# Taking 64 of 256 tokens out of the expert scans of a two-model kernel and gathering their expert rows by index

## The chip, the core and the metric

The kernel runs on one core of one Trainium2 chip. The metric is the time of one execution of the whole program in microseconds (us); the median of three runs is compared. The core has a matrix engine (PE, with its weight loads shown as PEld), three elementwise engines (DVE = VectorE, ACT = ScalarE, POOL = GpSimd), a queue for transfers (SP), and 16 DMA engines that all queues share.

## The reference, cut to what matters

Two transformer models run one after the other on 256 tokens of width 1024, two layers each. The change is in the last part of each layer of the first model, a layer of 16384 experts: every token picks 8 x 16 = 128 experts, takes the dot product of its normed input with each one's `down` row, and adds up their `up` rows, weighted.

```
def peer_ffn(x, w_query, sub_keys, down, up):
    ...
    idx = jnp.take_along_axis(cand_i, pos, axis=-1)     # per token 8 heads x 16 experts
    gate = jax.nn.softmax(top_s, axis=-1)

    def expert_block(args):
        xb, ib, gb = args
        a = jnp.einsum('thkd,td->thk', down[ib], xb).astype(jnp.float32)
        c = (gb * jax.nn.gelu(a)).astype(up.dtype)
        return jnp.einsum('thk,thkd->td', c, up[ib]).astype(x.dtype)
    ...
```

## The kernel before

Nothing is gathered before the change. The function `peer` computes the dot products of all 256 tokens with all 16384 `down` rows as a dense matrix product, multiplies them by a matrix of gates that is zero except where a token chose an expert, and multiplies the result with all `up` rows, again dense. All of this is in 32-bit floats split into two parts: a weight tile `wr` (128 x 1024, 512 KB) is fetched by SP, ACT rounds it to `wh` (line 255), DVE forms the rest `wl` (line 256), and `mm3` (lines 303 to 305) issues three matmuls for each 128 x 128 block. So one weight tile stands for 24 matmuls, with the 256 tokens as the moving columns. `wr`, `wh` and `wl` have four buffers each.

Four stages follow each other in each of the two layers, with 64 weight tiles each:

- **First down scan**, `dscan(0)`: the first 8192 `down` rows. Beside it DVE does the routing (the top-k, the indices `ij`, the gates `gt`).
- **Second down scan**, `dscan(1)`: the other 8192. Beside it `build(0)` makes the gates of the first half in 32 blocks of 8 tokens. A block is three fp16 operations on DVE (line 1314 twice, line 1329 once), 16 small fp16 matmuls of one-hot matrices (line 1338), and one multiply of `ga` on DVE (line 1320).
- **First up scan**, `uscan(0)`: `ga` of the first half times the `up` rows. Beside it `build(1)`. `coef` (lines 293 and 294) splits `ga` for two weight tiles at a time.
- **Second up scan**, `uscan(1)`: the rest of the `up` rows, with nothing beside it. `tail` then adds the sums `accs` to the residual.

What runs beside a scan is a generator. After each weight tile `wt` calls `tick`, which adds a rate to a credit and lets the generator issue work until the costs that it yields have used the credit up (`R1`, `R2`, `R3` = 1150, 1500, 1600 a tile; a block of `build` yields 600 + 900 + 600). Each engine works through its own queue in order, and an instruction that has to wait holds up everything behind it on that engine. POOL has no part in the work before the change.

Of the kernel before, what the change touches and what calls it, by code (L numbers as in the profile page):

```python
# [23 lines left out]
F32 = mybir.dt.float32  # L24
# [3 lines left out]
U32 = mybir.dt.uint32  # L28
AF = mybir.ActivationFunctionType
OP = mybir.AluOpType  # L30
# [90 lines left out]
def prep(inp):  # L121
# [11 lines left out]
    for l in range(DEPTH):  # L133
# [14 lines left out]
        a[f"sk{l}"] = bd  # L148
        a[f"down{l}"] = np.ascontiguousarray(
            i["peer_down"][l].reshape(128, 128, 8, 128).transpose(0, 3, 2, 1)).reshape(128, 128, 1024)  # L150
        a[f"up{l}"] = np.ascontiguousarray(i["peer_up"][l]).reshape(128, 128, 1024)

        w = i["w_in_2"][l]
# [44 lines left out]
class K:  # L198
    def __init__(self, ctx, tc, ap, ahead):
        self.tc, self.nc, self.ap, self.ctx = tc, tc.nc, ap, ctx  # L200
        nc = self.nc
        self.P = ctx.enter_context(tc.tile_pool(name="keep", bufs=1))
        self.W = ctx.enter_context(tc.tile_pool(name="wts", bufs=1))
        self.S = ctx.enter_context(tc.tile_pool(name="scr", bufs=1))
        self.ps = ctx.enter_context(tc.tile_pool(name="psum", bufs=1, space=PSUM))
        self.dr = ctx.enter_context(tc.tile_pool(name="dram", bufs=1, space=DRAM))
        self.x = self.P.tile([128, 8, T], F32, name="xres", bufs=1)
        self.nw = self.P.tile([128, 13, 8], F32, name="nw")
        self.eps = self.P.tile([128, 1], F32, name="eps")
# [20 lines left out]
        self.todo, self.sqs = [], []  # L230

    def cap(self, name, rows=128):
        o, w = _COFF[name]
# [31 lines left out]


    def tick(self):
        self.credit += self.rate
# [141 lines left out]
    def tail(self, accs, rows, wi, scale=None):  # L410

        self.pre(wi)
        if wi == N_FIN:
# [5 lines left out]
        def done(d):  # L419
            s = slice(2 * d, 2 * d + 2)  # L420
            xs = self.x[:, s]
            if scale is None:
# [11 lines left out]
        self.lastrows(accs, rows, done)  # L434
        if wi != N_FIN:
            self.todo = self.norm_steps()
            return
# [38 lines left out]
    def colpair(self, srcs, xh, xl):  # L476
# [636 lines left out]
WARM = 14  # L1113
R1, R2, R3 = 1150, 1500, 1600
H1 = H2 = 0


def peer(k, l, nxt):
# [4 lines left out]
    with k.tc.tile_pool(name=f"peer_{l}", bufs=1) as p:  # L1123
# [5 lines left out]
        ga1 = p.tile([128, HI * T], F32, name="ga1")  # L1129
        top = ExitStack()  # L1130
        q = top.enter_context(k.tc.tile_pool(name=f"first_{l}", bufs=1))
        ga = [q.tile([128, HI * T], F32, name="ga0"), ga1]

        rt, off = ga[1], [HI * T - 13000]

        def rtile(*shape):
            n = 1
# [1 line left out]
                n *= s  # L1139
            a = rt[:, off[0]:off[0] + n]  # L1140
            off[0] += n
            assert off[0] <= HI * T
# [12 lines left out]
        nc.sync.dma_start(sk, ap[f"sk{l}"])  # L1155
        k.cols(ap[f"w_q{l}"], 0, 8, xh, xl, lambda j, m, ps: V.tensor_mul(qT[:, j:j + m], ps, k.rsb))

        for h in range(0, 8, 2):
            for tt in range(2):
                ps = k.pst("mx", [128, 2, 256])  # L1160
                for j in range(2):
                    nc.tensor.matmul(ps[:, j], qT[:, h + j, tt * 128:(tt + 1) * 128], sk, start=True, stop=True)  # L1162
                c = h + tt
                t = k.S.tile([128, 2, T], F32, name="sq", bufs=2)[:, 0]
                V.scalar_tensor_tensor(t, k.x[:, c], k.nw[:, N_FFN + l, c:c + 1], k.rs, op0=OP.mult, op1=OP.mult)
                k.split(xh[:, c], xl[:, c], t)
                nc.scalar.copy(sc[:, tt, h:h + 2], ps)
        TB = 8
        room = k.P.tile([128, 4096], F16, name="xres", bufs=1)
        sizes = (TB * 128, TB * HI, 2 * TB * HI)  # L1170
# [5 lines left out]

        def dscan(half, dst):
            def ev(j, m, ps):
                nc.scalar.activation(dst[:, j * T:(j + m) * T], ps[:, :m].rearrange("p a t -> p (a t)"), AF.Gelu_apprx_tanh)  # L1179
            k.cols(down, half * HI, HI, xh, xl, ev)  # L1180


        sv = rtile(2, 8, 2, 16)
# [14 lines left out]
        def routing():  # L1198
# [79 lines left out]
            for src, kind in ((ij[0], 0), (ij[1], 1), (gt, 2)):  # L1278
# [8 lines left out]
                else:  # L1287
# [3 lines left out]
                    V.tensor_copy(g3[:, :, 0], gb)  # L1291
                    V.tensor_sub(g3[:, :, 1], gb, g3[:, :, 0])

        k.beside(routing(), R1, H1)
        dscan(0, ga[0])

        sets = [[room[:, starts[i]:starts[i + 1]] for i in range(3)],
                [k.S.tile([128, sizes[0]], F16, name="sq", bufs=2), room[:, starts[3] + sizes[0]:starts[3] + sizes[0] + sizes[1]],
# [1 line left out]
        pairs = io16.rearrange("p (a d) -> p a d", d=2)  # L1300

        def build(half, dst):
            d3 = dst.rearrange("p (i t) -> p i t", t=T)
            hs = slice(half * HI, (half + 1) * HI)

            def parts(b):
# [37 lines left out]
        dscan(1, ga[1])  # L1344
        k.drain()
        accs = k.rows_begin()
        ring = [k.S.tile([128, 8, T], F32R, name=n, bufs=1) for n in ("xh", "xl")]
        end = []

        def at(i):  # L1350
            return [t[:, i % 8] for t in ring] if i < 2 * HI - 2 else [t[:, i % 2] for t in end]

        def coef(i):
            r, o = i % 8, i % HI * T
            h, lo = [t[:, r:r + 2] for t in ring] if i < 2 * HI - 2 else end
            k.split(h.rearrange("p a t -> p (a t)"), lo.rearrange("p a t -> p (a t)"), ga[i // HI][:, o:o + 2 * T])

        def uscan(half):
            for i in range(half * HI, (half + 1) * HI, 2):
# [2 lines left out]
                if i % HI + 2 < HI:  # L1362
                    coef(i + 2)
                if i == 2 * HI - 2:
                    k.tail(accs, [k.wt(ap[f"up{l}"][e]) + tuple(at(e)) for e in (i, i + 1)], nxt, scale=1.0 / GS)
                else:
                    for e in (i, i + 1):
                        k.row(accs, *k.wt(ap[f"up{l}"][e]), *at(e), e == 0, False)

        k.beside(build(1, ga[1]), R3, H2)  # L1370
        uscan(0)
        k.drain()
        top.close()
# [391 lines left out]
```

## Time and profile before

| | us |
|---|---|
| runs (three) | 2913.3, 2915.08, 2918.97 |
| median | 2915.08 |
| the profiled execution | 2919.18 |
| its span, first to last instruction | 2917.1 |
| PE busy in the span | 2889.8 (99%) |
| DVE busy | 2077.0 (71%) |
| ACT busy | 1457.7 (50%) |
| POOL busy | 0.2 |

The four stages of the first layer lie at 243 to 1015 us, those of the second at about 1236 to 2013 us. Busy time of PE is the union of pipelined records, so a busy PE only says that it never ran dry; how fast it goes is read from the distance between the starts of two matmuls. The granted clock is 0.994 on average, and 1.00 (the level of 2.4 GHz) in the stages above.

### The profile page before, as it was taken

How to read it: one execution, taken by the hardware profiler on the slowest of the kernel's cores; microseconds unless marked ns; L12 is line 12 of the kernel's file. 1: busy time of each engine (PE TensorE's matmuls, PEld its weight loads, DVE VectorE, ACT ScalarE, POOL GpSimd, SP SyncE). 2: the span in 40 equal slices, each digit the busy share in tenths (PEclk: the TensorE clock that was granted, in tenths of full speed). 3: DMA queues.
4: the chain of work that ended last, by engine and by line, in shares of the span. 5: the costliest groups of instructions: out<-in, count | busy, mean ns of one | idle time of the engine just before them, and what ended most of it. 6: DMA issues, size and time to landing. Idle time of an engine off the chain costs nothing.

```text
span 2917.1 us, 59823 instructions
## 1 busy us (share of the span) xinstructions
PE 2889.8 (99%) x25130; PEld 2836.1 (97%) x25130; DVE 2077.0 (71%) x3484; ACT 1457.7 (50%) x1963; POOL 0.2 (0%) x4
## 2 busy tenths in 40 slices
PE   9999999999999999999999999999999999999998
PEld 8989999999999989999999999999999999999998
DVE  7769978769755586798786895556667656667655
ACT  7655553443444476545434434444546544546544
POOL 0000000000000000000000000000000000000000
PEclk9999999999999999999999999999999999999999
DMA  6655554554555555555545445555455555455553
GB/s 202 182 171 168 182 179 163 166 171 160 188 181 184 179 171 181 176 178 184 169 163 172 163 160 195 182 184 189 153 173 188 179 183 179 162 186 181 174 182 129
DMA packets 150493, 511.50 MB, mean 175 GB/s; under 512 B 17176, under 2 KB 26520, under 8 KB 149200
## 3 DMA queue, kind: packets, MB, share of 16 engines
q1 hardware_dynamic: 145904, 503.02, 53.2%
q10 hardware_dynamic: 4320, 4.67, 0.5%
q8 instruction: 196, 3.21, 0.5%
q14 instruction: 73, 0.60, 0.1%
HBM read 500.23 MB, written 7.39 MB: 174 GB/s over the span
## 4 chain that ended last, share of the span: by engine, by line
PE 95%; ACT 2%; DMA 1%; DVE 1%; issue 0%; SPq 0%; ACTq 0%; DVEq 0%
PE col L303 18%; PE col L305 18%; PE col L304 18%; PE acc L303 12%; PE acc L304 12%; PE acc L305 12%; PE mx L1338 2%; ACT wh L255 1%; PE mx L1162 1%; DMA wr<-in_w_hi 0%; PE acc L658 0%; PE acc L1402 0%; DVE wl L256 0%; PE mx L341 0%; DMA c_tri<-in_consts 0%
## 5 line engine op out<-in xcount | busy, mean ns | idle before, releaser
L255 ACT CAST wh<-wr 128x1024 fp32r<-128x1024 f32 (+1 forms) x922 | 960.3, 1044 | 1276.0 <-PE col L304 594.5
L256 DVE TENSOR_TENSOR wl<-wr,wh 128x1024 fp32r<-128x1024 f32 (+1 forms) x922 | 1120.4, 1217 | 608.1 <-ACT wh L255 605.4
L303 PE MATMUL col<-xh,wh 128*128 128x256 f32 x3856 | 1104.7, 286 | 2.3 <-ACT silg L1574 0.9
L305 PE MATMUL col<-xh,wl 128*128 128x256 f32 x3856 | 1096.1, 284 | 4.6 <-DVE wl L256 4.6
L304 PE MATMUL col<-xl,wh 128*128 128x256 f32 x3856 | 1094.7, 284 | 0.0
L305 PEld LDWEIGHTS col<-xh,wl 128*128 128x128 f32 x3856 | 741.7, 192 | 6.8 <-DVE wl L256 5.4
L303 PEld LDWEIGHTS col<-xh,wh 128*128 128x128 f32 x3856 | 742.0, 192 | 4.5 <-ACT silg L1574 1.7
L304 PEld LDWEIGHTS col<-xl,wh 128*128 128x128 f32 x3856 | 742.0, 192 | 0.1
L303 PE MATMUL acc<-xh,wh 128*128 128x256 f32 x2016 | 574.4, 285 | 2.1 <-ACT xh L293 2.1
L304 PE MATMUL acc<-xl,wh 128*128 128x256 f32 x2016 | 570.5, 283 | 0.0
L305 PE MATMUL acc<-xh,wl 128*128 128x256 f32 x2016 | 570.1, 283 | 0.0
L303 PEld LDWEIGHTS acc<-xh,wh 128*128 128x128 f32 x2016 | 386.4, 192 | 2.4 <-ACT xh L293 2.4
L304 PEld LDWEIGHTS acc<-xl,wh 128*128 128x128 f32 x2016 | 387.1, 192 | 0.0
L305 PEld LDWEIGHTS acc<-xh,wl 128*128 128x128 f32 x2016 | 386.9, 192 | 0.0
L1320 DVE TENSOR_TENSOR ga<-ga,mx 128x512 f32<-128x512 f32 x128 | 87.3, 685 | 41.5 <-PE mx L1338 39.5
L304 PE MATMUL acc<-fl,wh 128*128 128x256 f32 x352 | 98.1, 279 | 0.0
L305 PE MATMUL acc<-fh,wl 128*128 128x256 f32 x352 | 98.0, 279 | 0.0
L303 PE MATMUL acc<-fh,wh 128*128 128x256 f32 x352 | 97.7, 280 | 0.0
L294 DVE TENSOR_TENSOR xl<-ga,xh 128x512 fp32r<-128x512 f32 x126 | 85.7, 683 | 0.0
L293 ACT CAST xh<-ga 128x512 fp32r<-128x512 f32 x126 | 76.9, 615 | 0.0
L1179 ACT ACTIVATE ga<-col 128x512 f32<-128x512 f32 x128 | 75.7, 592 | 0.0
L303 PE MATMUL col<-wh,xh 128*128 128x512 f32 (+3 forms) x192 | 70.7, 372 | 3.4 <-ACT hg L1076 2.0
(466 smaller groups left out, 3420.0 us busy)
## 6 DMA issues: line engine op xcount, KB each, us to landing
wr<-in_down SPq DMA_DIRECT2D x256, 512.0 KB, 3.5
wr<-in_up SPq DMA_DIRECT2D x256, 512.0 KB, 3.9
wr<-in_w SPq DMA_DIRECT2D x132, 512.0 KB, 3.9
wr<-in_w_in SPq DMA_DIRECT2D x106, 512.0 KB, 4.0
wr<-in_xa_k SPq DMA_DIRECT2D x16, 512.0 KB, 4.0
wr<-in_xa_v SPq DMA_DIRECT2D x16, 512.0 KB, 4.3
wr<-in_w_out SPq DMA_DIRECT2D x16, 512.0 KB, 3.4
wr<-in_w_q SPq DMA_DIRECT2D x16, 512.0 KB, 3.5
```

The lines of the kernel that those rows point to most:

```text
L255: nc.scalar.copy(h[:, :w], r[:, :w])
L256: self.lows.append(nc.vector.tensor_sub(l[:, :w], r[:, :w], h[:, :w].bitcast(F32)).ins.name)
L293: self.nc.scalar.copy(h, src)
L294: self.nc.vector.tensor_sub(l, src, h.bitcast(F32))
L303: mm(ps, ah, bh, start=first, stop=False, skip_group_check=True)
L304: mm(ps, ah, bl, start=False, stop=False, skip_group_check=True)
L305: mm(ps, al, bh, start=False, stop=last, skip_group_check=True)
L1162: nc.tensor.matmul(ps[:, j], qT[:, h + j, tt * 128:(tt + 1) * 128], sk, start=True, stop=True)
L1179: nc.scalar.activation(dst[:, j * T:(j + m) * T], ps[:, :m].rearrange("p a t -> p (a t)"), AF.Gelu_apprx_tanh)
L1320: V.tensor_mul(dv, dv, ps.rearrange("p t i -> p i t"))
L1338: nc.tensor.matmul(ps[:, t], oj[:, t], gi[:, t, q], start=q == 0, stop=q == 1, skip_group_check=True)
```

## The change

Tokens 192 to 255 (`GN` = 64) leave the dense scans, which now have `TD` = 192 moving columns. For each of them the 128 chosen rows of `down` and of `up` are fetched by index. The 64 tokens x 128 experts are spread on 128 partitions, two partitions to a token, so there are `NG` = 64 gathers of 128 `down` rows (512 KB each) and 64 of `up` rows in each layer. A gather is an indirect DMA that POOL issues into one of four buffers `grow`. A `down` gather is reduced on DVE against the token's input `xg` (line 1367). Of each three `up` gathers two are scaled in place on ACT (line 1380) and added to `pacc` on POOL (line 1381), and one is scaled and added to `gacc` on DVE (line 1384). `gsel` then folds the two partitions of a token into `accs` with small matmuls (line 1449). A second generator, `other`, runs beside the first; its rate is `GR2` = 600 in the second down scan, `GR3` = 500 in the first up scan and `GR4` = 3000 in the second up scan, where a `down` row costs 1200, an `up` row for POOL 400 and one for DVE 1200. What is left is issued before the last sums.

```diff
     def tick(self):
+        if self.other is not None:
+            self.lent += self.orate
+            while self.other is not None and self.lent > 0:
+                c = next(self.other, None)
+                ...
+                    self.lent -= c
...
-                self.coltile(ps[:, j], h, l, xh, xl)
+                self.coltile(ps[:, j, :xh.shape[2]], h, l, xh, xl)
...
+GN = 64
+TD = T - GN
+RS = 128 // GN
+NG = 128 // RS
+NB = 4
+PSH = (2, 3)
+GR2, GR3, GR4 = 600, 500, 3000
...
-                k.split(xh[:, c], xl[:, c], t)
+                k.split(xh[:, c, :TD], xl[:, c, :TD], t[:, :TD])
+                nc.scalar.copy(t2[:, :128].rearrange("p (s t) -> p s t", s=RS), t[:, None, TD:].to_broadcast([128, RS, GN]))
+                nc.tensor.matmul(px[c // 4][:, c % 4 * 128:c % 4 * 128 + 128], t2[:, :128], k.ident, start=True, stop=True,
+                                 skip_group_check=True)
...
+        k.drain()
+
+        def gathered():
+            tabs = [ap[f"rows{l}"], ap[f"up{l}"].rearrange("a b c -> (a b) c")]
+            rows = []
+            def get(n):
+                if n < 2 * NG:
+                    r = p.tile([128, D], F32, name="grow", bufs=NB)
+                    nc.gpsimd.indirect_dma_start(out=r, out_offset=None, in_=tabs[n // NG],
+                                                 in_offset=bass.IndirectOffsetOnAxis(ap=gix[:, n % NG:n % NG + 1], axis=0))
+                    rows.append(r)
+            for n in range(NB - 1):
+                get(n)
+            for g in range(NG):
+                get(g + NB - 1)
+                r = rows.pop(0)
+                V.tensor_tensor_reduce(r, r, xg, 1.0, 0.0, OP.mult, OP.add, gav[:, g:g + 1])
+                ...
+                yield 1200
+            ...
+            for g in range(NG):
+                get(NG + g + NB - 1)
+                r = rows.pop(0)
+                c = gav[:, g:g + 1]
+                if PSH and g % PSH[1] < PSH[0]:
+                    nc.scalar.mul(r, r, c)
+                    nc.gpsimd.tensor_add(pacc, pacc, r)
+                    yield 400
+                else:
+                    V.scalar_tensor_tensor(gacc, r, c, gacc, op0=OP.mult, op1=OP.add)
+                    yield 1200
+        k.other, k.orate = gathered(), GR2
...
-            n = T // TB
+            n = TD // TB
...
+        def more(d):
+            if d == 0:
+                while k.other is not None:
+                    k.lent = 1e9
+                    k.tick()
+            gs = [gacc, pacc] if PSH else [gacc]
+            for j in range(2):
+                for i, g in enumerate(gs):
+                    nc.tensor.matmul(accs[d][:, j, TD:], g[:, (2 * d + j) * 128:(2 * d + j + 1) * 128], gsel, ...)
...
+            k.split(h[:, :, :TD], lo[:, :, :TD], ga[i // HI][:, o:o + 2 * TD].rearrange("p (a t) -> p a t", a=2))
...
         k.beside(build(1, ga[1]), R3, H2)
+        k.orate = GR3
         uscan(0)
...
+        k.orate = GR4
         uscan(1)
```

On ACT, where the second up scan of the first layer begins, before the change (`wr` to `wh` is a weight tile, `ga` to `xh` the rounding of coefficients for two tiles; numbers tell buffers apart):

```order
L293 CAST xh_7600<-ga0_2297 128x512
L255 CAST wh_10078<-wr_10076 128x1024
L255 CAST wh_10108<-wr_10106 128x1024
L293 CAST xh_7600<-ga0_2297 128x512
L255 CAST wh_10140<-wr_10138 128x1024
L293 CAST ch_10262<-ga1_2293 128x512
L255 CAST wh_10170<-wr_10168 128x1024
L293 CAST xh_7600<-ga1_2293 128x512
```

ACT alternates between weight tiles and coefficients, and goes on so to the end of the stage. On ACT a few tiles into the same stage after the change (`grow` is an `up` row for each partition, scaled in place by its weight `gav`):

```order
L257 CAST wh_10162<-wr_10160 128x1024
L257 CAST wh_10201<-wr_10199 128x1024
L303 CAST xh_7575<-ga1_2293 128x2x192
L1380 ACTIVATE grow_10172<-grow_10172,gav_2299 128x1024
L1380 ACTIVATE grow_10205<-grow_10205,gav_2299 128x1024
L1370 ACTIVATE gav_2299<-gav_2299 128x16
L257 CAST wh_10241<-wr_10239 128x1024
L1380 ACTIVATE grow_10247<-grow_10247,gav_2299 128x1024
L1380 ACTIVATE grow_10251<-grow_10251,gav_2299 128x1024
L257 CAST wh_10292<-wr_10290 128x1024
L303 CAST xh_7575<-ga1_2293 128x2x192
L1380 ACTIVATE grow_10258<-grow_10258,gav_2299 128x1024
```

The 43 scalings of the layer stand within 18 successive weight tiles, two or three ahead of each; behind them ACT's queue again has only weight tiles and coefficients.

On POOL, at the same place after the change (before it, POOL's queue held only its start-up):

```order
L1358 DMA grow_10169<-in_rows0,gix_2297 128x1024
L1358 DMA grow_10172<-in_up0,gix_2297 128x1024
L1358 DMA grow_10205<-in_up0,gix_2297 128x1024
L1381 ISA
L1381 TENSOR_TENSOR pacc_2296<-pacc_2296,grow_10172 128x1024
L1358 DMA grow_10208<-in_up0,gix_2297 128x1024
L1358 DMA grow_10247<-in_up0,gix_2297 128x1024
L1358 DMA grow_10251<-in_up0,gix_2297 128x1024
L1381 TENSOR_TENSOR pacc_2296<-pacc_2296,grow_10205 128x1024
L1358 DMA grow_10255<-in_up0,gix_2297 128x1024
L1358 DMA grow_10258<-in_up0,gix_2297 128x1024
L1381 TENSOR_TENSOR pacc_2296<-pacc_2296,grow_10247 128x1024
```

Gathers of `up` rows and the adds of earlier ones now share this queue, one behind the other: three gathers to two adds.

## Rows read from the trace of the kernel before

**Rows 1.** The page: busy time by engine, and the chain that ended last.

```profile
PE 2889.8 (99%) x25130; PEld 2836.1 (97%) x25130; DVE 2077.0 (71%) x3484; ACT 1457.7 (50%) x1963; POOL 0.2 (0%) x4
PE 95%; ACT 2%; DMA 1%; DVE 1%; issue 0%; SPq 0%; ACTq 0%; DVEq 0%
```

**Rows 2.** Stages of layer one: length, PE, PEld, DVE, ACT, POOL, clock, DMA share, GB/s.

```profile
246.00:430.00 184.00, 184.00 (x1548) 183.96 (x1547) 158.72 (x471) 93.27 (x104) 0.00 (x0) 1.00 0.57 184
430.00:626.00 196.00, 196.00 (x2006) 194.67 (x2005) 143.87 (x189) 80.19 (x94) 0.00 (x0) 1.00 0.52 167
626.00:815.00 189.00, 187.93 (x1920) 186.56 (x1917) 156.09 (x214) 80.28 (x95) 0.00 (x0) 1.00 0.53 171
830.00:1010.00 180.00, 180.00 (x1503) 180.00 (x1502) 94.21 (x92) 79.11 (x90) 0.00 (x0) 1.00 0.58 184
```

**Rows 3.** PE timeline (start, us): 256-column matmuls around four of one column.

```profile
208.73 0.28 PE L305 MATMUL col<-xh,wl 128*128 128x256 f32 x1
208.85 0.50 PE L341 MATMUL mx<-ones,sq 128*128 128x1 f32 x4
209.21 0.36 PE L303 MATMUL col<-xh,wh 128*128 128x256 f32 x1
209.41 0.28 PE L304 MATMUL col<-xl,wh 128*128 128x256 f32 x1
209.53 0.28 PE L305 MATMUL col<-xh,wl 128*128 128x256 f32 x1
```

**Rows 4.** Timeline of PEld, the weight loads of the same place.

```profile
208.74 0.53 PEld L341 LDWEIGHTS mx<-ones,sq 128*128 128x128 f32 x4
209.19 0.19 PEld L303 LDWEIGHTS col<-xh,wh 128*128 128x128 f32 x1
209.30 0.19 PEld L304 LDWEIGHTS col<-xl,wh 128*128 128x128 f32 x1
```

**Rows 5.** Timeline of PE: matmuls with 512 moving columns.

```profile
25.07 0.40 PE L303 MATMUL col<-wh,xh 128*128 128x512 f32 x1
25.77 0.40 PE L303 MATMUL col<-wh,xh 128*128 128x512 f32 x1
```

**Rows 6.** Timeline of PE: the 16 records of one block of gates.

```profile
429.18 0.64 PE L1338 MATMUL mx<-xres 128*128 128x64 f16 x16
429.66 0.36 PE L303 MATMUL col<-xh,wh 128*128 128x256 f32 x1
```

**Rows 7.** Timeline of DVE in the first up scan.

```profile
635.26 0.68 DVE L1314 TENSOR_TENSOR xres<-io,jS 128x1024 f16<-128x1024 f16 x1
635.86 1.22 DVE L256 TENSOR_TENSOR wl<-wr,wh 128x1024 fp32r<-128x1024 f32 x1
637.00 0.42 DVE L1314 TENSOR_TENSOR xres<-io,rstd 128x512 f16<-128x512 f16 x1
637.33 0.68 DVE L294 TENSOR_TENSOR xl<-ga,xh 128x512 fp32r<-128x512 f32 x1
637.94 0.68 DVE L1329 TENSOR_TENSOR xres<-xres 128x1024 f16<-128x1024 f16 x1
638.54 1.21 DVE L256 TENSOR_TENSOR wl<-wr,wh 128x1024 fp32r<-128x1024 f32 x1
```

**Rows 8.** Timeline of ACT in the second up scan, with its waits.

```profile
981.20 1.05 ACT L255 CAST wh<-wr 128x1024 fp32r<-128x1024 f32 x1 [1.31 <-PE acc L304]
```

**Rows 9.** SP's issue (ns min/median/max); the page's row, us to landing.

```profile
L244 SPq DMA_DIRECT2D wr<-in_up x256: 327/328/328, 607.6 to 1989.8; - x128
wr<-in_up SPq DMA_DIRECT2D x256, 512.0 KB, 3.9
```

**Rows 10.** Groups of DVE, 246 to 430 us: a small two-input operation.

```profile
L1213 DVE TENSOR_TENSOR ga<-ga 128x128 f32<-128x128 f32 x4 | 1.0, 280 | 0.0
```

**Rows 11.** Windows, line 341 alone (PE, PEld): the highest DMA rate read.

```profile
208.85:209.18 0.33, 0.33 (x4) 0.33 (x4) 1.00 0.96 397
```

**Rows 12.** Groups of PE: matmuls in plain 32-bit floats, two records each.

```profile
L1162 PE MATMUL mx<-ga 128*128 128x256 f32 x64 | 15.2, 387 | 0.0
```

More of the change, by code (lines that the diff above doesn't have):

```diff
@@ L150, in prep @@
             i["peer_down"][l].reshape(128, 128, 8, 128).transpose(0, 3, 2, 1)).reshape(128, 128, 1024)
+        a[f"rows{l}"] = np.ascontiguousarray(i["peer_down"][l])
         a[f"up{l}"] = np.ascontiguousarray(i["peer_up"][l]).reshape(128, 128, 1024)
@@ L230, in __init__ @@
         self.todo, self.sqs = [], []
+        self.other, self.orate, self.lent = None, 0.0, 0.0
     def cap(self, name, rows=128):
@@ L267, in tick @@
     def tick(self):
+        if self.other is not None:
+            self.lent += self.orate
+            while self.other is not None and self.lent > 0:
+                c = next(self.other, None)
+                if c is None:
+                    self.other, self.lent = None, 0.0
+                else:
+                    self.lent -= c
         self.credit += self.rate
@@ L408, in lastrows, with tail @@
             done(d)
-    def tail(self, accs, rows, wi, scale=None):
+    def tail(self, accs, rows, wi, scale=None, part=None, more=None):
         self.pre(wi)
@@ L421, in done @@
             xs = self.x[:, s]
+            if more is not None:
+                more(d)
             if scale is None:
@@ L432, in done @@
             self.pre_pair(d)
-        self.lastrows(accs, rows, done)
+        self.lastrows(part or accs, rows, done)
         if wi != N_FIN:
@@ L1141, in rtile @@
             off[0] += n
-            assert off[0] <= HI * T
+            assert off[0] <= HI * TD + 712
             if len(shape) > 1:
@@ L1156, in peer @@
         k.cols(ap[f"w_q{l}"], 0, 8, xh, xl, lambda j, m, ps: V.tensor_mul(qT[:, j:j + m], ps, k.rsb))
+        px = [k.pst("acc") for _ in range(2)]
         for h in range(0, 8, 2):
@@ L1163, in peer @@
                 c = h + tt
-                t = k.S.tile([128, 2, T], F32, name="sq", bufs=2)[:, 0]
+                t2 = k.S.tile([128, 2, T], F32, name="sq", bufs=2)
+                t, t2 = t2[:, 0], t2[:, 1]
                 V.scalar_tensor_tensor(t, k.x[:, c], k.nw[:, N_FFN + l, c:c + 1], k.rs, op0=OP.mult, op1=OP.mult)
-                k.split(xh[:, c], xl[:, c], t)
+                k.split(xh[:, c, :TD], xl[:, c, :TD], t[:, :TD])
+                nc.scalar.copy(t2[:, :128].rearrange("p (s t) -> p s t", s=RS), t[:, None, TD:].to_broadcast([128, RS, GN]))
+                nc.tensor.matmul(px[c // 4][:, c % 4 * 128:c % 4 * 128 + 128], t2[:, :128], k.ident, start=True, stop=True,
+                                 skip_group_check=True)
                 nc.scalar.copy(sc[:, tt, h:h + 2], ps)
+        for i in range(2):
+            nc.scalar.copy(xg[:, 512 * i:512 * i + 512], px[i])
         TB = 8
@@ L1178, in ev @@
             def ev(j, m, ps):
-                nc.scalar.activation(dst[:, j * T:(j + m) * T], ps[:, :m].rearrange("p a t -> p (a t)"), AF.Gelu_apprx_tanh)
-            k.cols(down, half * HI, HI, xh, xl, ev)
+                nc.scalar.activation(dst[:, j * TD:(j + m) * TD].rearrange("p (a t) -> p a t", a=m), ps[:, :m, :TD],
+                                     AF.Gelu_apprx_tanh)
+            k.cols(down, half * HI, HI, xh[:, :, :TD], xl[:, :, :TD], ev)
         sv = rtile(2, 8, 2, 16)
@@ L1292, in routing @@
                     V.tensor_sub(g3[:, :, 1], gb, g3[:, :, 0])
+            pick = rtile(128)
+            nc.scalar.copy(pick.rearrange("p (s t) -> p s t", s=RS), k.ident[:, None, 128 - GN:].to_broadcast([128, RS, GN]))
+            V.scalar_tensor_tensor(ij[1][:, 1], ij[0][:, 1], 128.0, ij[1][:, 1], op0=OP.mult, op1=OP.add)
+            ps = k.pst("mx")
+            for i, src in enumerate((ij[1], gt)):
+                nc.tensor.matmul(ps[:, i * 128:i * 128 + 128], pick, src[:, 1].rearrange("p h k -> p (h k)"),
+                                 start=True, stop=True, skip_group_check=True)
@@ L1294, in peer @@
+            for s in range(RS):
+                pr = slice(s * GN, s * GN + GN)
+                pv = ps[pr].rearrange("p (c g s) -> p c g s", g=NG, s=RS)
+                V.tensor_copy(gix[pr], pv[:, 0, :, s])
+                nc.scalar.mul(gga[pr], pv[:, 1, :, s], GS)
+            yield 1000
+        V.tensor_add(gsel, k.ident[:, 0:GN], k.ident[:, GN:2 * GN])
+        for s in range(2, RS):
+            V.tensor_add(gsel, gsel, k.ident[:, s * GN:s * GN + GN])
         k.beside(routing(), R1, H1)
@@ L1346, in peer @@
         accs = k.rows_begin()
+        part = [a[:, :, :TD] for a in accs]
+        def more(d):
[6 more added lines that the diff above has]
+                for i, g in enumerate(gs):
+                    nc.tensor.matmul(accs[d][:, j, TD:], g[:, (2 * d + j) * 128:(2 * d + j + 1) * 128], gsel,
+                                     start=i == 0, stop=i == len(gs) - 1, skip_group_check=True)
         ring = [k.S.tile([128, 8, T], F32R, name=n, bufs=1) for n in ("xh", "xl")]
@@ L1350, in at @@
         def at(i):
-            return [t[:, i % 8] for t in ring] if i < 2 * HI - 2 else [t[:, i % 2] for t in end]
+            return [t[:, i % 8, :TD] for t in ring] if i < 2 * HI - 2 else [t[:, i % 2, :TD] for t in end]
         def coef(i):
-            r, o = i % 8, i % HI * T
+            r, o = i % 8, i % HI * TD
             h, lo = [t[:, r:r + 2] for t in ring] if i < 2 * HI - 2 else end
-            k.split(h.rearrange("p a t -> p (a t)"), lo.rearrange("p a t -> p (a t)"), ga[i // HI][:, o:o + 2 * T])
+            k.split(h[:, :, :TD], lo[:, :, :TD], ga[i // HI][:, o:o + 2 * TD].rearrange("p (a t) -> p a t", a=2))
         def uscan(half):
@@ L1364, in uscan @@
                 if i == 2 * HI - 2:
-                    k.tail(accs, [k.wt(ap[f"up{l}"][e]) + tuple(at(e)) for e in (i, i + 1)], nxt, scale=1.0 / GS)
+                    k.tail(accs, [k.wt(ap[f"up{l}"][e]) + tuple(at(e)) for e in (i, i + 1)], nxt, scale=1.0 / GS,
+                           part=part, more=more)
                 else:
                     for e in (i, i + 1):
-                        k.row(accs, *k.wt(ap[f"up{l}"][e]), *at(e), e == 0, False)
+                        k.row(part, *k.wt(ap[f"up{l}"][e]), *at(e), e == 0, False)
         k.beside(build(1, ga[1]), R3, H2)
+        k.orate = GR3
         uscan(0)
```

22 lines of the change are left out of this document (18 added, 4 removed).

## The prediction

> **What bounds the kernel now.** I read the page first: PE is busy 99% of the span and 95% of the chain that ended last [rows 1], so time is won only where PE's stream gets shorter, and lost where it is held up. Then the windows of the four stages: PE never runs dry, the clock is 1.00, while DVE is busy 159 of 184 us in the first down scan, 144 of 196 and 156 of 189 in the two with gates, and 94 of 180 in the last; POOL does nothing; DMA engines are 52 to 58% busy [rows 2]. So a stage is a stream of matmuls 0.12 us apart, start to start [rows 3]: 24 to a weight tile give 2.88 us, 64 tiles 184 us. A block of gates adds 0.48 us [rows 6], 32 of them 15. The layer's four stages sum to 184 + 200 + 200 + 184 = 768 us.
>
> **What sets the 0.12 us.** This decides what 192 columns instead of 256 are worth. The starts of 512-column matmuls lie (25.77 - 25.07)/3 = 0.233 us apart [rows 5], so 256 more columns cost 0.113 us, and by columns alone 192 would take 0.12 - 64 x 0.113/256 = 0.092 us. But a matmul also needs its own weights, and these take time too: with a single moving column, four loads take 209.19 - 208.74 = 0.45 us, 0.112 each; the next load, of the kind the scans use, is followed by another after 0.11; and there the next matmul comes 0.20 us after the one before instead of 0.12, since its load was not hidden [rows 3, 4]. At 256 columns the load fits just behind the moving columns; at 192 it no longer does. I take **0.112 us**: 2.69 us a tile. A quarter fewer columns then bring 7% and not 23%.
>
> **The change part by part, one layer.**
>
> *First down scan.* 64 x (2.88 - 2.69) = 12 us less. DVE's 159 us [rows 2] still fit into 172.
>
> *Second down scan.* DVE forms a weight tile's rest in 1.14 us, and the four operations of a block take 0.60 + 0.33 + 0.60 + 0.60 = 2.13, start to start [rows 7], with line 1320 taken like line 1314. The rate of 1500 against 2100 a block makes 0.71 block a tile, the new rate of 600 against 1200 half a `down` row a tile, which I price like the weight tile's two-input pass over 1024 elements, 1.14. DVE: 1.14 + 1.52 + 0.57 = 3.23 us a tile; PE: 2.69 + 0.71 x 0.48 = 3.03. DVE leads while there are gates to build: 24 blocks instead of 32, 33.6 tiles, 109 us; the other 30.4 tiles at 2.69 are 82. Sum 191 against 200: 9 less.
>
> *First up scan.* 0.76 block, 0.42 row and half a coefficient split (0.61 us for 512 elements [rows 7], 0.46 for 384) make 1.14 + 1.62 + 0.48 + 0.23 = 3.47 us a tile for 31.5 tiles, 109 us, then 32.5 x 2.69 = 87: 196 against 200, 4 less.
>
> *Edges.* The eight small transposes of the 64 tokens and the 16 products that fold the gathered sums are plain-float matmuls of two records, 48 x 0.112 = 5 us on PE. Index work on DVE is some ten small operations and lies in the first down scan's slack; the copies to `xg` add about a us. 6 more.
>
> *Second up scan.* Here the gathers of `up` come: 64 of them stand inside the queues of 18 weight tiles, on ACT two or three ahead of each tile, on DVE one. Neither engine can pass a row that has not landed, so the weight tiles behind wait, and PE with them; its head start is the four buffers of `wh` and `wl`. The length B of this stretch is what the rows need, not what PE needs. Their slowest link is POOL, which issues each gather and adds two of three, one behind the other. Neither operation is in the trace. **Issue of a gather:** SP spends 0.33 us on a transfer of the same size, and 3.9 us pass until it lands [rows 9]; if POOL were held for all of it, that is the upper end. I take 1.1, the middle of the two in ratio. **An add on POOL:** DVE's pass over 1024 takes 1.22 us [rows 7]; the dearest DVE row per element, 280 ns for 128 [rows 10], would make 2.24. Since nothing shows POOL at DVE's pace, I take 2.24. B = 64 x 1.1 + 43 x 2.24 = **167 us**. ACT is no limit: 43 scalings and 18 tiles at 1.05 [rows 8] are 64 us. Around the stretch stand 46 tiles, less the four of head start: 42 x 2.69 = 113. The stage takes 280 us against 184: **96 more**.
>
> By the Trainium skill (GPSIMD Engine Reference, section 3.1) a two-input add takes 1.96 times as long on GpSimd as on VectorE; no row here shows it. By that, 2.39 an add, the stage would take 6 us longer and the result would be about 3082.
>
> *Sum.* 12 + 9 + 4 - 6 = 19 less, 96 more: 77 more a layer, 154 in both. On the profiled execution, 2919.2 (2.1 outside its span), this gives 3073; the median of the runs is 4 lower: **3069 us**.
>
> *Ends.* The cheapest B: the loop through four buffers, (0.33 + 3.9 + 1.05 + 1.22)/4 = 1.63 us a row, makes 104; 82 transfers of 0.524 MB at the highest rate that a window shows, 397 GB/s [rows 11], make 108. With 108 the stage is 37 longer, the layer 18, the kernel 2951. The dearest: 64 x 3.9 + 43 x 2.24 = 346 us, the stage 275 longer, the kernel 3427. So as long as the load sets the pace, no price of POOL ends below 2951.
>
> **Rivals.**
>
> *The columns set the pace, and the rows come fast (faster).* If a load of the next weights hides wholly behind 192 columns, a matmul takes 0.092 us, a tile 2.21. The first down scan is then held by DVE's 159 us (25 less), the others come to 109 + 67 and 109 + 72 us (24 and 19 less), and the last stage is B + 46 x 2.21 - 9 = B + 93. It is faster than before from B under 184 + 68 - 6 - 93 = 153 us down; at 108 it saves 45 a layer: 2825. For it: the line through 256 and 512 columns fits [rows 3, 5]. Against it: the exposed loads [rows 3, 4], and that B must be low as well. With B = 167 it would be 2943, slower.
>
> The Trainium skill (TensorE: Matmul & The Clock Gate, section "Back-to-back issue gap") gives an isolated gap of the columns over 2.4 plus 2.5 ns, 82.5 ns for 192. At 256 this would be 109 where the trace has 120, so the rule is short here; by it, and with B = 108, the result would be near 2775.
>
> *The transfers set the pace of the rows.* POOL is as quick as the cheapest rows and B is about 108: 2951. For it: DMA engines have over 40% free. Against it: adds and gathers share one queue.
>
> *The narrow matmul is dear.* No matmul of this split kind in the trace has under 256 columns. If below that it fell back to the pace of plain floats (15.2 us for 32 matmuls, 0.475 each at 256 columns [rows 12]), 192 would take 0.36, and 12288 of them would add about 2900 us. Nothing in the trace hints at it.
>
> *DVE and POOL hold each other up*, so that B passes the dear end: above 3430.
>
> **How the numbers follow.** Load sets the pace and POOL the rows: 0.63. Transfers set the rows: 0.13, of which 0.02 ends within 0.2% and 0.02 faster, if the stages with gates give a little more than the sum has. Columns set the pace: 0.17, of which 0.09 ends faster, 0.01 within 0.2% and 0.07 slower. Narrow matmul: 0.03; mutual hold-up: 0.04. So faster by over 0.2% (about what a measurement of this kernel can tell from no change) 0.11, within 0.03, slower 0.86. Below 2900 lie the 0.09 in which columns and rows are both quick; above 3380, where B is about 322 us, the 0.07 of the last two cases and some 0.03 of the first. The range is 2900 to 3380.
>
> **What would show it.** In the profile after: starts of the 192-column matmuls 0.11 apart, not 0.09. In the second up scan a stretch of 110 to 300 us in which PE is mostly idle, its releaser `wh` or `wl`, these behind line 1380 or 1384, and these behind the landing of `grow`, with POOL busy throughout; after it 43 tiles at 2.69. The second down scan and first up scan near 191 and 196 us with DVE over 95% busy in their first halves. The prediction is wrong if POOL issues and adds in under 1.7 us a row and a weight load is not the floor; and its size is wrong by 2 x 64 us for each us that a row costs more or less on POOL.

## The result and the profile after

The changed kernel takes **3176.22 us** (median, 3173.94 to 3179.72) beside 2914.4 us for the kernel before on the same chip: 1.0896 times as long, with an interval of 1.0877 to 1.0915. The forecast of slower holds, and the time lies inside the range, 107 us above the predicted 3069.

The page of the profile after, its parts on busy time, the 40 slices, the chain, and the costliest groups:

```profile
PE 2897.0 (91%) x24722; PEld 2826.3 (89%) x24722; DVE 2245.6 (71%) x3672; ACT 1534.1 (48%) x2086; POOL 505.2 (16%) x348
PE   9999999999545999999999996459999999999998
...
POOL 0000011111786000000111116880000000000000
PEclk9999999999666999999999997559999999999999
...
PE 55%; issue 23%; POOL 11%; DVE 4%; DMA 3%; ACT 3%; POOLq 0%; ACTq 0%; DVEq 0%; SPq 0%
...
L1380 ACT ACTIVATE grow<-grow,gav 128x1024 f32<-128x1024 f32 x86 | 98.7, 1148 | 283.6 <-DMA grow<-in_up,gix 283.4
L1381 POOL TENSOR_TENSOR pacc<-pacc,grow 128x1024 f32<-128x1024 f32 x86 | 209.9, 2441 | 14.6 <-ACT grow L1380 12.6
...
L1358 POOL DMA_INDIRECT grow<-in_up,gix x128 | 154.3, 1206 | 45.5 <-issue 19.1
```

PE was busy 99% of the span before, and made up 95% of the chain [rows 1]. Now two holes stand in its row, one in each layer, just where POOL's row is full. Busy time of PE hardly tells this: it is 7 us higher than before with 408 fewer matmuls, since a matmul in the holes lasts longer.

Windows of the first layer's three first stages, and of the last one in three pieces (columns as in [rows 2]):

```profile
239.58:420.98 181.40, 176.25 (x1549) 175.67 (x1548) 160.29 (x498) 90.11 (x106) 5.87 (x5) 0.98 0.62 192
420.98:609.14 188.16, 186.07 (x1954) 185.43 (x1952) 165.84 (x229) 81.24 (x102) 32.40 (x32) 1.00 0.83 272
609.14:802.73 193.59, 187.76 (x1888) 186.70 (x1889) 172.29 (x249) 79.57 (x98) 31.43 (x28) 0.98 0.77 250
808.60:1010.00 201.40, 93.98 (x408) 86.87 (x408) 84.35 (x48) 69.20 (x70) 175.21 (x105) 0.58 0.63 206
1010.00:1030.00 20.00, 17.51 (x130) 17.27 (x131) 13.08 (x12) 9.95 (x14) 2.10 (x1) 0.79 0.58 187
1030.00:1139.60 109.60, 109.60 (x984) 109.60 (x984) 59.81 (x65) 49.93 (x63) 0.00 (x0) 1.00 0.63 192
```

The second up scan, 184 us before, is now 337 us long (802.73 to 1139.62), 335 in the second layer. For 201 of them, from the first scaling of an `up` row to the last, PE gets through 408 matmuls, 17 weight tiles; POOL is busy for 175. Some 20 us after the rows are done, PE runs without a gap again. From the first matmul of a stage to the first of the next, the stages stand so (us; layer one, and layer two where it differs):

| stage | before | after | change | predicted |
|---|---|---|---|---|
| up to the first down scan | 224.7 / 217.7 | 231.6 / 224.7 | +7 | +6 |
| first down scan | 190.7 | 181.4 | -9 | -12 |
| second down scan | 204.1 | 188.2 | -16 | -9 |
| first up scan | 200.9 | 193.6 / 194.7 | -7 / -6 | -4 |
| second up scan | 184.2 | 336.9 / 335.0 | +153 / +151 | +96 |

The sum is +127 and +126, 253 of the 257 us by which the two spans differ. The first two rows belong together: 25 records of small products (line 1162 before, 1189 after), some 5 us, lay behind the first matmul of the first down scan before the change and lie ahead of it now. The +6 that was predicted for the first row also holds the matmuls that fold the sums, and these stand in the last row.

The waits from 803 to 1010 us (engine, line and what it waited for, us in total, times, longest):

```profile
ACT grow L1380 <- DMA grow<-in_up,gix: 141.8, 42, 9.6
DVE gacc L1384 <- DMA grow<-in_up,gix: 86.2, 16, 6.9
...
PE acc L313 <- ACT wh L257: 65.9, 16, 6.5
...
PE acc L315 <- DVE wl L258: 36.3, 17, 5.4
...
POOL grow L1358 <- issue: 9.1, 27, 1.7
POOL grow L1358 <- DVE gacc L1384: 8.4, 6, 1.6
POOL pacc L1381 <- ACT grow L1380: 6.1, 1, 6.1
```

This is the predicted chain: PE waits for `wh` and `wl`, whose engines stand at rows that have not landed. POOL waits for other engines only some 15 us.

### The profile page after: what moved, and what is told of

Same layout as the page of the kernel before. It is cut to its first block, busy times and chain, and to the rows that moved or that the text cites. A ratio compares the mean times of both kernels' runs of the same rounds, so it can differ in the third digit from the quotient of the medians.

```text
span 3174.3 us, 60070 instructions
## 1 busy us (share of the span) xinstructions
PE 2897.0 (91%) x24722; PEld 2826.3 (89%) x24722; DVE 2245.6 (71%) x3672; ACT 1534.1 (48%) x2086; POOL 505.2 (16%) x348
## 4 chain that ended last, share of the span: by engine, by line
PE 55%; issue 23%; POOL 11%; DVE 4%; DMA 3%; ACT 3%; POOLq 0%; ACTq 0%; DVEq 0%; SPq 0%
PE col L313 12%; PE col L315 11%; PE col L314 11%; POOL grow L1358 7%; PE acc L313 6%; PE acc L315 6%; PE acc L314 6%; POOL pacc L1381 4%; DMA grow<-in_up,gix 2%; DVE wl L258 2%; ACT wh L257 1%; PE mx L1189 0%; PE acc L670 0%; DMA wr<-in_w_hi 0%; PE acc L1510 0%
## 5 line engine op out<-in xcount | busy, mean ns | idle before, releaser
L313 PE MATMUL col<-xh,wh 128*128 128x192 f32 (+1 forms) x3856 | 1085.1, 281 | 16.1 <-ACT ga L1212 11.8
L315 PE MATMUL col<-xh,wl 128*128 128x192 f32 (+1 forms) x3856 | 1078.2, 280 | 3.4 <-DVE wl L258 3.4
L314 PE MATMUL col<-xl,wh 128*128 128x192 f32 (+1 forms) x3856 | 1077.4, 279 | 0.0
L313 PE MATMUL acc<-xh,wh 128*128 128x192 f32 x2016 | 598.0, 297 | 154.8 <-ACT wh L257 153.1
L315 PE MATMUL acc<-xh,wl 128*128 128x192 f32 x2016 | 596.3, 296 | 66.9 <-DVE wl L258 66.9
L314 PE MATMUL acc<-xl,wh 128*128 128x192 f32 x2016 | 592.5, 294 | 3.4 <-DVE xl L304 3.4
L1358 POOL DMA_INDIRECT grow<-in_rows,gix x128 | 138.9, 1085 | 1049.8 <-DVE gav L1367 647.9
L1381 POOL TENSOR_TENSOR pacc<-pacc,grow 128x1024 f32<-128x1024 f32 x86 | 209.9, 2441 | 14.6 <-ACT grow L1380 12.6
L1358 POOL DMA_INDIRECT grow<-in_up,gix x128 | 154.3, 1206 | 45.5 <-issue 19.1
L1367 DVE CUSTOM_DVE_ANT_0 grow<-grow,xg 128x1024 f32<-128x1024 f32 x128 | 156.0, 1221 | 2.1 <-DMA grow<-in_rows,gix 2.1
```

Of the source, the lines that this page charges most:

```text
L313: mm(ps, ah, bh, start=first, stop=False, skip_group_check=True)
L314: mm(ps, ah, bl, start=False, stop=False, skip_group_check=True)
L315: mm(ps, al, bh, start=False, stop=last, skip_group_check=True)
L1358: nc.gpsimd.indirect_dma_start(out=r, out_offset=None, in_=tabs[n // NG], in_offset=bass.IndirectOffsetOnAxis(ap=gix[:, n % NG:n % NG + 1] ...
L1367: V.tensor_tensor_reduce(r, r, xg, 1.0, 0.0, OP.mult, OP.add, gav[:, g:g + 1])
L1381: nc.gpsimd.tensor_add(pacc, pacc, r)
```

## Experiments

Each kernel is the changed kernel with the edit shown. Its time is the median, the ratio is to the kernel before on the same chip (2916.3 and 2917.2 us in the two sets).

### What narrower matmuls give without the rows

```diff
-        k.other, k.orate = gathered(), GR2
+        V.memset(gacc, 0.0)
+        nc.gpsimd.memset(pacc, 0.0)
```

> No row is gathered: the sums of the 64 tokens are set to zero, so their expert part is left out of the result; the scans with 192 columns, the index work and the final small matmuls stay. It prices the gain alone. Theory A: the scans take 64 x 24 x 0.112 = 172 us each plus 12 us for the gates in two of them, 2 x (12 + 16 + 16 + 12) - 21 = 91 us less than before: 2815 to 2835 us. Rival (the gathers of the down rows already cost what the narrower matmuls would give): well below, 2750 or less, since by columns alone a scan would take 141 us.

2831.57 us, 0.9703 [0.9687, 0.9720]. The stages are 181.1, 186.6, 184.1 and 175.0 us. A window of the last one:

```profile
791.00:966.00 175.00, 175.00 (x1570) 175.00 (x1569) 94.83 (x100) 80.91 (x99) 0.00 (x0) 1.00 0.63 193
```

Besides the 1536 matmuls of the scan it holds 32 records of small ones, which fold the gathered sums at its end. So the scans without the 64 tokens are worth 85 us in all, and the rows turn that into a loss of 262.

The second kernel also cuts the second up scan to 128 columns:

```diff
+                elif i >= HI:
+                    for e in (i, i + 1):
+                        k.row([a[:, :, :128] for a in accs], ..., *[t[:, :128] for t in at(e)], ...)
```

> As the kernel without gathers, but in the second up scan only 128 moving columns (64 further tokens' part of it is left out of the result). It prices the weight load by itself. If a load of weights takes 0.112 us and is the floor, the starts of the matmuls there stay 0.11 us apart, and the stage and the kernel take the same time as with 192 columns, within 5 us. If the moving columns set the pace, the starts are 0.064 us apart and the stage is 70 us shorter in each layer, held only by DVE and ACT at 1.2 us a tile.

2833.09 us in one run, the second up scan again 175.03 us. PE's timeline in the changed kernel after its rows (192 columns), and then in this one (128):

```profile
1079.83 0.27 PE L313 MATMUL acc<-xh,wh 128*128 128x192 f32 x1
1079.94 0.27 PE L314 MATMUL acc<-xl,wh 128*128 128x192 f32 x1
```

```profile
899.76 0.28 PE L315 MATMUL acc<-xh,wl 128*128 128x128 f32 x1
899.87 0.28 PE L313 MATMUL acc<-xh,wh 128*128 128x128 f32 x1
```

Both start 0.11 us apart, so at 192 columns something other than the columns sets the pace. What is left is the weight load, for which the exposed loads before the change spoke already [rows 3, 4]. It is not a floor under every matmul: the 16 small fp16 matmuls of a block of gates, each with a weight load of its own, took 0.48 us together [rows 6]. That the load itself takes the 0.11 us is argued from these rows; no run changes the load.

### What the stretch consists of

All rows on DVE, as crowded as before; POOL only issues, ACT has no row:

```diff
-PSH = (2, 3)
+PSH = None
```

> All up rows are scaled and added on DVE, none on ACT and POOL; the rate stays 3000, so the 64 rows stand within some 27 tiles. Theory A with POOL as the slowest link: POOL only issues, 64 x 1.2 = 77 us, DVE's part is 64 x 1.28 + 27 x 1.4 = 120 us, transfers 91 x 0.524 MB at some 300 GB/s are 160 us; the stretch is 110 to 160 us, the stage 225 to 270 us instead of 336 and the kernel 2955 to 3045 us. Theory B (landings are late in any case): over 3120 us.

3009.93 us, 1.0317 [1.0292, 1.0343]; the second up scan is 255 and 249 us. A row costs 1200 of the generator's credit here against 667 on average, so the rows spread over some 25 weight tiles and take 146 us (809 to 955). A window, and waits from 810 to 955 us:

```profile
850.00:900.00 50.00, 36.90 (x214) 35.39 (x212) 38.97 (x36) 10.03 (x12) 27.36 (x22) 0.74 0.90 324
```

```profile
ACT wh L257 <- DMA wr<-in_up: 98.2, 21, 7.1
POOL grow L1358 <- DVE gacc L1384: 49.0, 34, 3.8
```

POOL is idle for nearly half of the window. ACT now waits for the weight tile itself, with the DMA engines 90% busy at 324 GB/s: POOL is no longer the limit, and the transfers are near theirs. That they alone set the 146 us is not shown, since a later kernel moves 382 GB/s. The stage is 82 us shorter than in the changed kernel: 55 from the shorter stretch, 27 because more tiles lie inside it and fewer behind.

The other way round, POOL's adds are left out (so two thirds of the `up` rows are missing in the sums), and ACT still scales:

```diff
                     nc.scalar.mul(r, r, c)
-                    nc.gpsimd.tensor_add(pacc, pacc, r)
```

> The changed kernel without POOL's adds (two thirds of the up rows of the 64 tokens are left out of the result; they are still gathered and scaled on ACT), rate 3000. Theory: POOL's 43 adds of 2.44 us are over half of the 202 us stretch. Without them POOL only issues (64 x 1.2 = 77 us) and the transfers set the pace, as in the run with all rows on DVE (146 us); the stretch is 120 to 155 us, the stage 235 to 270 us, the kernel 2980 to 3050 us. Rival (the adds run in the shadow of the landings): the stretch stays above 185 us and the kernel above 3130 us.

3092.9 us in one run, between the two expectations: both missed. The second up scan is 296 and 293 us. The stretch shrinks from 201 to some 154 us (809 to 963), as expected; but with as many rows to a weight tile as before, nearly as many tiles are still to do behind it, and these 137 us had been set too low. Without the adds, POOL's issue waits for ACT (75 us in the first layer's stretch), ACT for landings (79). So the adds account for about 42 us of the stage's 153; who is next is near behind. This run also shows what the adds do to DVE. Groups of DVE (mean ns of one after the comma), 820 to 1000 us in the changed kernel, then 820 to 950 us without the adds:

```profile
L1384 DVE SCALAR_TENSOR_TENSOR gacc<-grow,gav,gacc 128x1024 f32<-128x1024 f32 x20 | 39.0, 1948 | 79.4 <-DMA grow<-in_up,gix 79.4
L258 DVE TENSOR_TENSOR wl<-wr,wh 128x1024 fp32r<-128x1024 f32 x16 | 26.8, 1676 | 25.2 <-ACT wh L257 25.2
L304 DVE TENSOR_TENSOR xl<-ga,xh 128x384 fp32r<-128x384 f32 x8 | 15.6, 1944 | 0.6 <-ACT xh L303 0.6
```

```profile
L1383 DVE SCALAR_TENSOR_TENSOR gacc<-grow,gav,gacc 128x1024 f32<-128x1024 f32 x19 | 24.4, 1283 | 5.7 <-DMA grow<-in_up,gix 5.7
L258 DVE TENSOR_TENSOR wl<-wr,wh 128x1024 fp32r<-128x1024 f32 x13 | 15.9, 1225 | 88.2 <-ACT wh L257 88.2
L304 DVE TENSOR_TENSOR xl<-ga,xh 128x384 fp32r<-128x384 f32 x6 | 3.3, 550 | 0.0
```

The same operations take 1.4 to 3.5 times as long beside the adds. In the changed kernel every one of these that starts while an add runs ends after that add: the rests of weight tiles and the rows 1.08 us after it or later, the splits of coefficients 0.42 (45 operations in both layers). The rival of a mutual hold-up was real, though not at the size that it was given.

### Spreading the rows over the whole scan

```diff
-GR2, GR3, GR4 = 600, 500, 3000
+GR2, GR3, GR4 = 600, 500, 800
```

> One number is changed: the rate of gathered rows in the second up scan is 800 a weight tile, not 3000, so the 64 up rows stand within some 60 tiles instead of 18. Theory A (crowding: rows stand in the queues of ACT and DVE faster than POOL can issue and add them, 202 us for 64 rows or 3.15 us a row in the changed kernel, and the weight tiles behind them wait): with about one row a tile the same 202 us lie beside 64 tiles of 2.69 us, the stage takes 205 to 225 us instead of 336, and the kernel 2930 to 2960 us. Theory B (the gathers land late, whatever stands where, because they share the DMA engines with the weight tiles): the waits on landings stay, at least 3100 us. Theory C (POOL's adds and DVE's two-input operations exclude each other, and cost DVE the time of every add): DVE gets 64 x 1.14 + 16 + 21 x 1.28 + 43 x 2.36 = 218 us of work in the stage, which is then the floor, so the kernel is not under 2940 us and the weight tile's rest on DVE takes over 1.5 us on average there.

3503.72 us, 1.2019 [1.1999, 1.2039]: far slower still, and the expectation fell. The second up scan is 501 us in both layers, with no engine near its limit (a window):

```profile
950.00:1000.00 50.00, 27.26 (x130) 25.38 (x131) 17.67 (x11) 12.47 (x14) 21.97 (x12) 0.60 0.33 120
```

Timelines of POOL, then of ACT, in this kernel:

```profile
953.72 1.64 POOL L1358 DMA_INDIRECT grow<-in_up,gix  x1 [0.27 <-POOL pacc L1381]
960.78 2.35 POOL L1381 TENSOR_TENSOR pacc<-pacc,grow 128x1024 f32<-128x1024 f32 x1 [5.42 <-ACT grow L1380]
963.40 1.64 POOL L1358 DMA_INDIRECT grow<-in_up,gix  x1 [0.27 <-POOL pacc L1381]
```

```profile
949.87 1.15 ACT L1380 ACTIVATE grow<-grow,gav 128x1024 f32<-128x1024 f32 x1 [9.51 <-DMA grow<-in_up,gix]
950.93 1.03 ACT L257 CAST wh<-wr 128x1024 fp32r<-128x1024 f32 x1
959.55 1.15 ACT L1380 ACTIVATE grow<-grow,gav 128x1024 f32<-128x1024 f32 x1 [7.18 <-DMA grow<-in_up,gix]
```

It is one round trip after another: issue 1.64, 4.2 to the landing (955.36 to 959.55), scaling 1.15, add 2.35, 0.27, then the next issue, 9.7 us in all. Buffers for three rows ahead exist, but the order does not use them. POOL's queue in this kernel (numbers tell buffers apart):

```
L1358 DMA grow_10433<-in_up0,gix_2297 128x1024
L1381 TENSOR_TENSOR pacc_2296<-pacc_2296,grow_10433 128x1024
L1358 DMA grow_10437<-in_up0,gix_2297 128x1024
L1358 DMA grow_10471<-in_up0,gix_2297 128x1024
L1381 TENSOR_TENSOR pacc_2296<-pacc_2296,grow_10437 128x1024
```

A gather stands directly before the add of its own row, so POOL stands at that add for a whole landing before it issues the next. On ACT the scaling of `grow_10791` stands ahead of `wh_10605`, although the code issues it some nine weight tiles later. The test is to forbid that: ACT's row work is ordered behind the weight tile after which it is issued.

```diff
-        nc.scalar.copy(h[:, :w], r[:, :w])
+        high = nc.scalar.copy(h[:, :w], r[:, :w]).ins.name
...
+        if self.other is not None:
+            for i in nc.cur_bb.bb.instructions[n:]:
+                if i.engine == mybir.EngineType.Activation:
+                    self.tc.add_manual_dep(i, high, ...)
...
+GR2, GR3, GR4 = 600, 500, 800
```

> As the run with the rate of 800, with one thing more: ACT's row work is kept behind the weight tile after which it is issued in the program. In the run with 800 alone the scalings stood some six weight tiles earlier in ACT's queue, and on POOL each gather came directly before its own add, so that a row cost one whole round of issue, landing, scaling and add (9.6 us between two scalings, 501 us for the stage). Here POOL's queue has three gathers ahead of each add again. Theory D (the round trip, because of the order of the queues): the rows fall back to POOL's pace of 3.15 us and lie beside 64 tiles, the stage takes 205 to 240 us and the kernel 2930 to 3000 us. Theory E (a row takes long to land whenever gathers are spread, or ACT and POOL are slowed by something else): at least 3300 us.

2984.61 us, 1.0230 [1.0213, 1.0247]: 519 us less than the kernel above by order alone. On POOL three other gathers now stand between a gather and its add, as in the changed kernel. The second up scan is 240 and 243 us, at the upper end of what was expected and still 65 over the 175 that PE needs. A window of it, and lines of DVE's and POOL's timelines (its lines are 5 higher from the pin on):

```profile
850.00:900.00 50.00, 39.36 (x289) 37.70 (x290) 47.15 (x25) 26.22 (x30) 45.27 (x27) 0.90 0.81 285
```

```profile
905.87 2.73 DVE L309 TENSOR_TENSOR xl<-ga,xh 128x384 fp32r<-128x384 f32 x1
```

```profile
903.94 1.64 POOL L1363 DMA_INDIRECT grow<-in_up,gix  x1 [0.27 <-POOL pacc L1386]
905.60 2.59 POOL L1386 TENSOR_TENSOR pacc<-pacc,grow 128x1024 f32<-128x1024 f32 x1
```

DVE's 0.55 us split of coefficients started inside an add and ended 0.4 us after it. In this window both engines are busy over 90%: POOL because of what it has to do, DVE because its work is stretched by POOL's (in the next two windows of 50 us DVE is busy for 41 and 42, POOL for 46 and 44). From the first scaling to the last it is 207 us, with POOL busy for 185, beside 201 and 175 in the changed kernel: the rows come no faster, but PE gets 54 weight tiles done beside them instead of 17. Which of the two engines keeps the stage at 240 us was not separated.

So the last two kernels keep POOL to its issues, put all rows on DVE, and spread them. First with the rates of the down scan and first up scan as they were:

```diff
-PSH = (2, 3)
-GR2, GR3, GR4 = 600, 500, 3000
+PSH = None
+GR2, GR3, GR4 = 600, 500, 1300
```

> All up rows on DVE and the rate 1300 a tile in place of 3000. DVE's queue keeps the program's order, so three gathers are under way. Crowding as the cause: DVE has 1.14 + 0.25 + 1.28 us a tile, just PE's 2.69, transfers 2 x 0.524 MB in 2.69 us are 390 GB/s, above the 315 that the run with all rows on DVE reached; so the transfers hold the stage at 128 x 0.524 MB / 315 GB/s = 213 us and the kernel is 2915 to 2950 us. If the transfers do not hold it: 175 us and 2840 to 2870 us. Rival (a spread does not help, as with POOL's rows): 3010 us or more.

**2874.1 us, 0.9855 [0.9839, 0.9871]**: 1.5% faster than before. The second up scan takes 177.7 and 177.4 us, 2.5 more than without any rows. Its window:

```profile
806.50:980.00 173.50, 170.26 (x1516) 169.50 (x1516) 165.80 (x163) 77.54 (x93) 97.92 (x62) 1.00 1.00 382
```

The DMA engines carry 382 GB/s, busy all the time, and DVE is busy 96% of it; PE still does not starve. So transfers do not hold this stage, and the time is 4 us above the band given for that case; but there is no room left: 64 rows and 64 tiles of 0.524 MB at 382 GB/s take 176 us.

In the other, no rows run while gates are being made:

```diff
-            self.lent += self.orate
+            self.lent += self.orate if self.side is None else 0.0
...
+GR2, GR3, GR4 = 1250, 1250, 1300
```

> All up rows on DVE; no rows while gates are built, one a tile (rate 1250) in the second halves of the second down scan and the first up scan, 1300 in the second up scan. Expected: the two stages with gates come down from 188 and 193 to 186 and 184 us, as without any gather, if one row a tile fits beside the weight tiles there; the second up scan as with rate 1300, 175 to 215 us. Kernel 2835 to 2925 us. Rival: the transfers of rows and tiles together (390 GB/s needed) hold all three second halves, and the kernel ends above 2925 us.

**2853.18 us, 0.9773 [0.9757, 0.9790]**, the fastest of all that were run with the whole computation. In the first layer the second down scan takes 186.7 us and the first up scan 184.2, as without rows; in the second layer the first up scan still takes 188.0. The second up scan gives 4 and 7 us back (181.4 and 184.4). Of the 85 us that narrower scans can give, this keeps 64.

## Why the prediction was right, and where its sizes were off

**The pace of a matmul: right.** The 192-column matmuls start 0.111 us apart in the median, where the load was taken as 0.112, and 128 columns change nothing. The rival in which columns set the pace (0.092) is refuted. The second up scan without rows still gains 9 us and not 12, because the 32 records that fold the sums now stand at its end: 1568 starts in 175.03 us are 0.112 each, against 0.120 before.

**The first down scan: a wait that the sum put at nothing.** DVE's 159 us do fit into the stage in total, but not in the order in which they stand. PE waits 5.2 us in this stage, nearly all for ACT, which stands at an operation of the routing that DVE has not yet fed (waits of PE from 239.6 to 421 us, then one line of ACT's timeline, changed kernel):

```profile
PE col L313 <- ACT ga L1212: 4.4, 2, 3.8
PE col L315 <- DVE wl L258: 0.8, 1, 0.8
```

```profile
352.15 3.70 ACT L1293 CAST ga<-ga 128x2048 f16<-128x2048 f32 x2 [6.70 <-DVE ga L1281]
```

The next two dozen matmuls start 0.21 us apart instead of 0.11, some 2.5 us more (granted clock 0.81 from 345 to 363 us). The kernel without rows shows the same wait (4.5 us), and PE had none in this stage before.

The Trainium skill (TensorE: Matmul & The Clock Gate, section "LDWEIGHTS (loading the stationary operand)") gives a load of 128 columns about 107 ns, which these gaps agree with to 4%. The Trainium skill's isolated gap of 82.5 ns for 192 columns (TensorE: Matmul & The Clock Gate, section "Back-to-back issue gap") is not reached in any stage here.

**The two stages with gates: right in kind, somewhat low.** DVE leads in their first halves as predicted (windows, columns as in [rows 2]):

```profile
421.00:520.00 99.00, 97.89 (x1122) 97.56 (x1120) 98.95 (x149) 39.57 (x49) 16.47 (x16) 1.00 0.79 248
609.00:710.00 101.00, 95.28 (x1039) 94.38 (x1040) 99.31 (x155) 37.55 (x47) 12.73 (x12) 0.97 0.68 212
```

The stages end at 188 and 194 us, where 191 and 196 were forecast. The rest of the difference is the length before, put at 200 and measured from matmul to matmul as 204 and 201.

**The second up scan: the right mechanism, 57 us too short.** The step that failed is B = 167 us; the stretch takes 201 in both layers. B was the sum of what POOL has to do, with no term for the time in which POOL stands. In layer one:

- An add was taken as 2.24 us and takes 2.44 (2.34 at the least): 43 x 0.20 = 8.6 more, of which 2 fall behind the stretch.
- An issue was taken as 1.1 us and takes 1.18 (1.21 over both layers; 0.93 at the least, 1.99 at most). The 62 of 64 that lie in the stretch take 72.5 us, 2 more than was counted for all.
- So POOL is busy for 175 us, 8 more than B. The other 26 are its idle time between instructions. The largest parts are the 9 us put down to issue and 8 for DVE to free a buffer (the waits above).

By the Trainium skill (GPSIMD Engine Reference, section 3.1) an add was put at 2.39 us; the traces agree, with 2.34 at the least and 2.44 in the mean.

This timeline of POOL and the one of DVE under it (changed kernel) show how the waits for DVE come about:

```profile
902.87 0.95 POOL L1358 DMA_INDIRECT grow<-in_up,gix  x1 [0.27 <-POOL pacc L1381]
903.84 2.35 POOL L1381 TENSOR_TENSOR pacc<-pacc,grow 128x1024 f32<-128x1024 f32 x1
907.55 1.69 POOL L1358 DMA_INDIRECT grow<-in_up,gix  x1 [1.36 <-DVE gacc L1384]
```

```profile
903.71 3.57 DVE L1384 SCALAR_TENSOR_TENSOR gacc<-grow,gav,gacc 128x1024 f32<-128x1024 f32 x1 [5.11 <-DMA grow<-in_up,gix]
907.20 1.21 DVE L258 TENSOR_TENSOR wl<-wr,wh 128x1024 fp32r<-128x1024 f32 x1
913.29 1.28 DVE L1384 SCALAR_TENSOR_TENSOR gacc<-grow,gav,gacc 128x1024 f32<-128x1024 f32 x1 [4.88 <-DMA grow<-in_up,gix]
```

DVE's row meets an add and takes 3.57 us instead of 1.28, ending 1.1 after the add; POOL's next gather needs that row's buffer and waits 1.36 for it.

The other 23 us lie around the stretch. PE does 47 tiles there, 2 ahead of it and 45 behind it, and not 42: 13 us more. The head start of four buffers did not show: 17 tiles are done in the stretch, not the 18 that stand in it and four more. The matmuls that fold the sums, counted under the edges, take 4 us at the end of this stage. The rest, some 5 us, goes with the first 20 us behind the rows, which held 130 matmuls instead of the 180 that fit at 0.111.

Of the 57 us the other stages of the layer gave back 6 (-25 against -19 in the table); twice the 51 that are left is nearly all of the 107 us by which the forecast was too low. That it lies in the range says little of this sum, since the range holds any B up to about 322 us.

**The rivals.** Transfers as the pace of the rows (B = 108) is refuted for the changed kernel, where the DMA engines are 63% busy in the stretch; it came near at 146 us once POOL's adds and ACT's rows were gone, with these engines 90% busy. The narrow matmul is not dear. The mutual hold-up exists and is part of the 26 us, but 3430 was far off.

So 85 us were won by the narrower scans and 345 lost to the rows, 322 of them in the second up scans: rows crowded into about 18 weight tiles in front of engines that work in order, paced by the slowest engine in their chain.

## What to carry to other kernels

Work that waits for a transfer, placed in an in-order queue ahead of what feeds PE, makes PE wait for it too: spread such rows over the stage, and read in the order whether gathers really stand rows ahead of their use, since buffers alone do not make them. Before an idle engine is given a share of the work, price its slowness in the chain and what it does to its neighbour; here leaving POOL's adds to a busy DVE was better by 300 us together with the spread. And before a dimension is cut, see whether the weight load is already the floor: a quarter fewer columns gave 7% of a matmul's pace (0.120 to 0.112 us) and not 25%.

## What the runs showed of the hardware that was not expected

- **DVE operations with two tensor inputs wait for an add on POOL.** Alone, the row operation takes 1.28 us and the 384-column split 0.55; beside the adds their means are 1.95 and 1.94, and one that starts during an add does not end before it. The Trainium skill (GPSIMD Engine Reference, section 1, "Specifications") says that the two engines share interfaces to SBUF and contend when a DVE instruction has two SBUF inputs; the trace agrees and gives the size.
- **A gather by index holds POOL for 0.93 us at the least, 1.2 in the mean and up to 1.99** (`up` rows, changed kernel), against the 0.33 that SP spends on as many bytes [rows 9]; it lands 4.2 us after its issue has ended (one case, in the spread kernel).
- **Gathers and plain loads together reached 382 GB/s over a whole stage**, with the DMA engines at a share of 1.00.
- **A starved PE is also slower at what it does get.** In the stretch the granted clock was 0.58, between the levels of 1.2 and 2.4 GHz but nearer the lower, with PE busy 94 of 201 us; matmuls of 192 columns started 0.21 us apart there (0.11 at a clock of 1.00). In the 20 us behind it the clock was 0.79. No engine waits for PE between 803 and 1010 us, so the low clock did not lengthen the stretch itself.
